# Gates of the mixer's merges as pairs of seven block products, and the modulation dots in the down parts

## The chip, the cores and the metric

The kernel runs on one core of one Trainium2 chip. The metric is the time of one execution on the device in microseconds (us). Before the change the median of three runs is 2345.42 us (2344.29 to 2346.27). A core has TensorE (PE, with its weight loads shown as PEld), VectorE (DVE), ScalarE (ACT), GpSimd (POOL) and SyncE (SP), which here issues nearly all DMAs. Each engine works off its own queue in order.

## The reference

Two layers, each of a feed-forward, a mixer and a second feed-forward on 512 tokens of 1024 channels in float32. Before each stands an RMS norm with a shift and a scale, behind it a gate, all three from `c @ w_ada + b_ada` (nine vectors of 1024 a layer, here called kinds 0 to 8: shift, scale, gate of each of the three sub-layers). The mixer, cut to what matters:

```python
proj = h @ w_in
qa, ka, va, ub, qc, kc, vc, f_lin, g_lin = jnp.split(proj, SPLIT_POINTS, axis=-1)
ya = chunked_relpos_attention(ha(qa), ha(ka), ha(va), qk_gain[0], qk_gain[1], rel_bias)
yb = multiscale_pool(ub, w_pool, pool_scale)          # windows 2, 4, 8, 16, one 128x128 map each
yc = forgetting_attention(hc(qc), hc(kc), hc(vc), qk_gain[2], qk_gain[3], f_lin + forget_bias)
ys = jnp.stack([ya, yb, yc], axis=2)
branch = jnp.einsum('bsnw,nwd->bsnd', ys, w_branch)   # three times 512 -> 1024
gates = jax.nn.sigmoid(g_lin.reshape(B, S, N_BRANCHES, D_MODEL))
merged = jnp.sum(gates * branch, axis=2)
return merged @ w_out
```

The gates `g_lin` are three products of 1024 x 1024 with the 512 tokens.

## The kernel before

**Precision.** Every large product is made from three matmuls (`triple`, L138): each operand is split into a high part, a copy to the matmul's float type by ScalarE, and a low part, the difference, by VectorE; high x high, high x low and low x high are added up in PSUM. A weight block of 128 x 1024 thus costs one ScalarE copy (L310) and one VectorE subtraction (L312), both in `wchunk`, which loads it through the tag "raw" (two buffers) and splits it into the tag "w" (three). The normed input is held split for good, as `hhi` and `hlo`: eight blocks of 128 channels by 512 tokens.

**Order.** The program is unrolled. A scheduler sets the order in each engine's queue from dependencies, free buffers and the order in which things are written. `later(delay, fn)` writes something down after so many 512-column matmuls of PE work (`pe`), at the next `poll`. `issue_after(ins)` puts an instruction behind `ins` on the same engine; `act_` and `vec_` chain everything that is passed to them in the written order on ScalarE and VectorE (`in_order`).

**Feed-forward.** 22 tiles of the hidden width are done in three parts of 6, 8 and 8. Where the gates and ups come in pairs of tiles, `stretch` computes them with the class `Seven` and `Blocks`: the weights of two tiles form a 2 x 2 block matrix (tile by half of the input channels), the input a 2 x 2 block matrix (half of the channels by half of the tokens), and seven block products with sums before and behind them replace eight (Strassen in Winograd's form). Each block product is `add_product` (L145), four times three matmuls of 256 columns. `Blocks` makes the sums of the input, `Seven` those of the weights: S1 and A11, S2, S3 and S4 and the second half, with their splits. Behind each gate and up part a down part follows (`k_outer`), in chunks of two tiles, for either half of the output.

**Modulation.** The rows of `w_ada` are loaded one by one (512 KB each, L220) and multiplied with the SiLU of c, spread over all partitions in `silc`, by one VectorE dot (L227). 16 rows are done at the start, 128 wait in `mod_queue`, in the order of the kinds. `side_work`, called with each weight chunk, adds `MOD_RATE` to a credit, and each whole credit draws a row, when `in_ffn` is set and the tag of the buffer, `mod_tag`, isn't "raw". `mod_need` draws what a later step needs at once. In `mod_dot` the dot is put behind the norm block written last (`after("norm")`), and the load behind the last weight load (`after("dma")`). Before, rows were drawn in the down parts (1.2 a chunk, into tag "v2") and in the merges of the mixer (1.2, into tag "b").

**Mixer.** Projections and the two attentions come first, with the attention branch's merge as filler of the second. Then `pool_in` projects the four groups of the pooling input; `pool_front` makes the window sums by doubling on VectorE, `pool_back` the small products. `merge_units` (L1217) goes through eight tiles of 128 output channels for the forgetting branch (n = 2) and eight for the pooling branch (n = 1): for each the gate, 8 x 3 matmuls of 512 columns, a tanh on ScalarE (L1238), the branch product, 4 x 3 matmuls, and `put_c` or `put_b`: VectorE multiplies (L1296), GpSimd adds to the merged block (L1297), and `put_b` also splits it for the output projection. That projection runs in two halves of four chunks; with its second half the next norm begins in two halves of the tokens (`Norm.front`, `Norm.back_start`, eight blocks `piece(d)` each, L404 to L407), while the first weights of the next feed-forward are loaded.

## Time and profile before

| | |
|---|---|
| median of three runs | 2345.42 us |
| the profiled execution | 2346.59 us |
| its span, first to last instruction | 2344.8 us |
| granted TensorE clock over the span | 1.000 |
| VectorE busy | 1749.1 us |
| dots of modulation rows into tag "b" (in the merges) | 57, 77.1 us of VectorE |
| dots into tag "v2" (start and down parts) | 87, 115.4 us of VectorE |
| GpSimd adds of the merges (L1297) | 32, 53.3 us |

The page sums the busy time of each engine over the span, and names groups of instructions by line, with count, sum and mean. Busy PE means that a matmul was under way; matmuls overlap at their ends, so the distance from start to start says what one costs in a stream. Views in order of time show start, length, engine, line and operands, and in brackets how long the engine was idle before and which instruction released it.

### The profile page before, as it was taken

Reading aid. Unit: us, or ns where it says so; the run is one execution under the profiler, and the core shown is the slowest. Engines: PE = TensorE matmul, PEld = TensorE weight load, DVE = VectorE, ACT = ScalarE, POOL = GpSimd, SP = SyncE. Lnnn points to the kernel's source line nnn. Section 1 sums busy time; section 2 is a strip of 40 time slices with the busy share of each in tenths; the row PEclk is TensorE's granted clock in tenths of the full one; section 3 lists DMA queues with packets and bytes.
Section 4 is the critical chain, followed back from the end, with each engine's and each line's share of the span. In section 5 each row is a group of like instructions: output and inputs, shape, how many; then the busy total and the mean of one; then the engine's idle time right before and its main releaser. Section 6 shows DMA issues by size and latency. Waiting matters only on the chain.

```text
span 2344.8 us, 37536 instructions
## 1 busy us (share of the span) xinstructions
PE 2315.3 (99%) x14322; PEld 2056.4 (88%) x14322; DVE 1749.1 (75%) x3042; ACT 1194.4 (51%) x2132; POOL 326.1 (14%) x433
## 2 busy tenths in 40 slices
PE   7999999999999999999999999999999999999999
PEld 5898998878888898989999989988788888999898
DVE  8887866787686577878687969677876865868593
ACT  5353555677632364635553636456765324636362
POOL 3000011244412110000000000112543112000000
PEclk9999999999999999999999999999999999999999
DMA  7625242333356524363325262533333655142322
GB/s 283 223 100 195 98 149 88 107 100 111 115 189 217 193 88 168 100 206 101 128 80 180 91 215 92 180 108 100 95 121 104 224 198 197 55 150 93 117 91 99
DMA packets 138137, 325.19 MB, mean 139 GB/s; under 512 B 13890, under 2 KB 16066, under 8 KB 137956
## 3 DMA queue, kind: packets, MB, share of 16 engines
q1 hardware_dynamic: 135266, 314.39, 39.7%
q0 software_dynamic: 2688, 8.39, 1.2%
q8 instruction: 113, 1.85, 0.3%
q14 instruction: 68, 0.56, 0.1%
q10 hardware_dynamic: 2, 0.00, 0.0%
HBM read 312.16 MB, written 6.38 MB: 136 GB/s over the span
## 4 chain that ended last, share of the span: by engine, by line
PE 50%; DVE 2%; ACT 2%; DMA 1%; issue 0%; POOL 0%; SPq 0%; ACTq 0%; DVEq 0%; POOLq 0%
PE acc L140 9%; PE acc L142 9%; PE acc L141 9%; PE acc L151 3%; PE acc L149 3%; PE acc L150 3%; PE mm L149 3%; PE mm L150 3%; PE mm L151 3%; PE mm L142 2%; PE mm L140 2%; PE mm L141 2%; PE mm L1111 0%; DVE w L312 0%; DMA v<-in_w_ada_dram 0%
## 5 line engine op out<-in xcount | busy, mean ns | idle before, releaser
L310 ACT CAST w<-raw 128x1024 fp32r<-128x1024 f32 (+1 forms) x255 | 264.4, 1041 | 268.1 <-PE acc L142 184.0
L312 DVE TENSOR_TENSOR w<-raw,w 128x1024 fp32r<-128x1024 f32 x247 | 312.8, 1270 | 116.6 <-ACT w L310 114.2
L140 PE MATMUL acc<-b,w 128*128 128x512 f32 (+1 forms) x960 | 360.1, 375 | 0.1
L142 PE MATMUL acc<-b,w 128*128 128x512 f32 (+1 forms) x960 | 356.4, 371 | 0.2 <-DVE w L312 0.2
L141 PE MATMUL acc<-b,w 128*128 128x512 f32 (+1 forms) x960 | 356.3, 371 | 0.0
L142 PEld LDWEIGHTS acc<-b,w 128*128 128x128 f32 x960 | 180.5, 188 | 32.3 <-DVE w L312 0.6
L140 PEld LDWEIGHTS acc<-b,w 128*128 128x128 f32 x960 | 180.4, 188 | 30.7 <-DVE xv L467 0.6
L141 PEld LDWEIGHTS acc<-b,w 128*128 128x128 f32 x960 | 180.4, 188 | 29.7
L140 PE MATMUL acc<-hhi,w 128*128 128x512 f32 x480 | 191.9, 401 | 2.5 <-ACT hhi L838 1.7
L142 PE MATMUL acc<-hhi,w 128*128 128x512 f32 x480 | 188.4, 393 | 2.0 <-DVE w L312 2.0
L141 PE MATMUL acc<-hlo,w 128*128 128x512 f32 x480 | 188.2, 392 | 2.1 <-DVE hlo L841 2.1
L140 PE MATMUL acc<-w,hhi 128*128 128x512 f32 x336 | 138.7, 414 | 0.9 <-ACT t L940 0.9
L142 PE MATMUL acc<-w,hlo 128*128 128x512 f32 x336 | 131.8, 392 | 0.0
L141 PE MATMUL acc<-w,hhi 128*128 128x512 f32 x336 | 131.7, 392 | 0.0
L227 DVE CUSTOM_DVE_ANT_0 v<-v,b,badac 128x1024 f32<-128x1024 f32 x87 | 115.4, 1339 | 17.1 <-DMA v<-in_w_ada_dram 17.1
L467 DVE SCALAR_TENSOR_TENSOR xv<-acc,badac,xv 128x512 f32<-128x512 f32 (+1 forms) x112 | 77.2, 690 | 67.7 <-PE acc L142 67.7
L557 DVE TENSOR_TENSOR ptb<-pta,ptb 128x1024 fp32r<-128x1024 f32 x70 | 85.7, 1224 | 50.9 <-ACT ptb L556 49.8
L149 PE MATMUL mm<-b,ptb 128*128 128x256 f32 x420 | 116.9, 278 | 1.8 <-ACT mm L610 1.8
L150 PE MATMUL acc<-b,ptb 128*128 128x256 f32 x420 | 116.1, 276 | 0.0
L151 PE MATMUL acc<-b,ptb 128*128 128x256 f32 x420 | 116.0, 276 | 0.0
L149 PE MATMUL acc<-b,ptb 128*128 128x256 f32 x420 | 116.0, 276 | 0.0
L150 PE MATMUL mm<-b,ptb 128*128 128x256 f32 x420 | 116.0, 276 | 0.0
(315 smaller groups left out, 6710.1 us busy)
## 6 DMA issues: line engine op xcount, KB each, us to landing
raw<-in_w_down_dram SPq DMA_DIRECT2D x88, 512.0 KB, 3.8
v<-in_w_ada_dram SPq DMA_DIRECT2D x87, 512.0 KB, 4.9
b<-in_w_ada_dram SPq DMA_DIRECT2D x57, 512.0 KB, 4.7
raw<-in_w_ubg_dram SPq DMA_DIRECT2D x56, 512.0 KB, 3.5
raw<-in_w_qkv_dram SPq DMA_DIRECT2D x42, 512.0 KB, 3.7
v<-in_w_gate_dram SPq DMA_DIRECT2D x70, 256.0 KB, 3.7
v<-in_w_up_dram SPq DMA_DIRECT2D x70, 256.0 KB, 3.2
raw<-in_w_gate_dram SPq DMA_DIRECT2D x70, 256.0 KB, 3.1
```

The costliest lines, as they stand in the source:

```text
L140: mm(o, lh, rh, start=start, stop=False)
L141: mm(o, lh, rl, start=False, stop=False)
L142: mm(o, ll, rh, start=False, stop=stop)
L149: mm(o, lh, rh, start=start and k == 0, stop=False, skip_group_check=True)
L150: mm(o, lh, rl, start=False, stop=False, skip_group_check=True)
L151: mm(o, ll, rh, start=False, stop=k == 3, skip_group_check=True)
L227: dot = nc.vector.tensor_tensor_reduce(out=raw, in0=raw, in1=silc[0], scale=1.0, scalar=badac[:, l, j, d:d + 1], op0=ALU.mult, op1=ALU.add ...
L310: nc.scalar.copy(hi, raw)
L312: lo_eng.tensor_tensor(lo, raw, hi.bitcast(F32), op=ALU.subtract)
L467: nc.vector.scalar_tensor_tensor(x, acc_j, gate, x, op0=ALU.mult, op1=ALU.add)
L557: vec_(lambda: nc.vector.tensor_tensor(pair[1], src, pair[0].bitcast(F32), op=ALU.subtract))
```

## The change

Per layer the gates of tiles 2 to 7 of the forgetting branch and of all eight tiles of the pooling branch are made in pairs by `merge_pairs`; tiles 0 and 1 of the forgetting branch stay with `merge_units`. `Blocks` is built while the pooling input is projected, and the first `Seven` during the direct tiles. The fronts and backs of the pooling groups are placed by hand: fronts between the two branch products of the first three pairs (`behind`), backs in the middle of the next pair's products (`between`), and all their VectorE and ScalarE steps are chained. No modulation rows are drawn in the merges; the down parts draw 1.9 a chunk, the last one 1.0 through the tag "pta" (one buffer), the mixer's projections 0.7, the output projection 1.0. Kind 7 comes ahead of kind 6, and `Ffn.run` asks for the shift of its norm itself. `silc` is loaded again behind the merges.

```diff
     def mod_step(l, j, d, tag="raw"):
-        raw = st([P, D], F32, tag, {"v2": 4, "raw": NRAW, "b": NB}[tag])
+        raw = st([P, D], F32, tag, {"v2": 4, "raw": NRAW, "b": NB, "pta": 1}[tag])
...
+    KINDS = (0, 1, 2, 3, 4, 5, 7, 6, 8)
...
-        return min(len(mod_queue), (l * 9 + j) * 8 + count - 16)
+        return min(len(mod_queue), (l * 9 + KINDS.index(j)) * 8 + count - 16)
...
         def run(self, nxt):
             l, s, ms = self.l, self.s, self.ms
+            if self.norm is not None:
+                mod_need(l, 3 * ms)
...
-                MOD_RATE[0] = 1.2
+                MOD_RATE[0] = 1.9
...
                         nxt.prefetch("v2")
-                        mod_tag[0] = "raw"
+                        mod_tag[0], MOD_RATE[0] = "pta", 1.0
...
     def pool_front(l, g, u):
...
-            nc.vector.tensor_tensor(nx[:, 16:], cur[:, 16:], cur[:, 16 - step:T + 16 - step], op=ALU.add)
+            vec_(lambda nx=nx, cur=cur, step=step: nc.vector.tensor_tensor(
+                nx[:, 16:], cur[:, 16:], cur[:, 16 - step:T + 16 - step], op=ALU.add))
...
-        b = st([P, 2, T], F32R, "ptb", 2)
-        split_to(b[:, 0, :], b[:, 1, :], df)
+        b = blk("b")
+        act_(lambda: nc.scalar.copy(b[:, 0, :], df))
+        vec_(lambda: nc.vector.tensor_tensor(b[:, 1, :], df, b[:, 0, :].bitcast(F32), op=ALU.subtract))
...
+    def merge_pairs(l, jobs, first, blocks):
...
+        todo = [first, Seven(gates(*jobs[1][:2]), ENTRY, stag="v2")]
+        for q, (n, d, ys, put, between, behind) in enumerate(jobs):
+            now = todo.pop(0)
+            nxt = todo[0] if todo else None
+            x, y, w = [acc((P, HALF)) for _ in range(3)]
...
+            go(x, "A11", "B11", True)
+            if nxt:
+                nxt.s1()
+            snap(y, x)
+            if nxt:
+                nxt.a11()
+                nxt.s234()
+            go(w, "S1", "T1", True)
+            snap(c[:, 2], w)
+            go(x, "S2", "T2", False)
+            snap(c[:, 0], x)
+            raw = st([P, 2, 4, P], F32, "raw", NRAW)
+            nc.sync.dma_start(raw, w_branch[l, n, d:d + 2].rearrange("a p k c -> p a k c"))
+            wb = duo((2, 4, P))
+            snap(wb[0], raw)
+            tens(wb[1], raw, wb[0].bitcast(F32), ALU.subtract)
+            if nxt:
+                nxt.pair12()
+            if q + 2 < len(jobs):
+                todo.append(Seven(gates(*jobs[q + 2][:2]), ENTRY, stag="v2"))
+            go(y, "A12", "B21", False)
+            go(x, "S3", "T3", False)
+            snap(c[:, 1], x)
+            for step in between:
+                step()
+            go(w, "S4", "B22", False)
+            tens(c[:, 1], c[:, 1], c[:, 2], ALU.add)
+            tens(c[:, 0], w, c[:, 0], ALU.add)
+            tanh(0, 0, y)
+            tanh(0, 1, c[:, 0])
+            if nxt:
+                nxt.pair34()
+            go(x, "A22", "T4", False)
+            tanh(1, 0, x)
+            tanh(1, 1, c[:, 1])
+            if nxt:
+                nxt.second()
+            for i in range(2):
+                pb = mmt()
+                for k in range(4):
+                    triple(pb, wb[0][:, i, k, :], wb[1][:, i, k, :], ys[k][:, 0, :], ys[k][:, 1, :], k == 0, k == 3)
+                put(d + i, pb, th[i])
+                if i == 0:
+                    for step in behind:
+                        step()
...
     class Mixer:
         def run(self, nxt):
-            in_ffn[0] = False
+            mod_tag[0], MOD_RATE[0] = "pta", 0.7
...
+            in_ffn[0] = False
             finish_turns()
...
             def put_b(d, pb, th):
                 put_c(d, pb, th)
-                b = blk("v2" if d < 4 else "b")
-                split_to(b[:, 0, :], b[:, 1, :], m[d // 2][:, d % 2, :])
-                mh.append(b)
+                if waiting:
+                    split_merged()
+                mh.append(blk("v2" if d == 5 else "b"))
+                waiting.append((m[d // 2][:, d % 2, :], mh[-1]))
...
+            blocks = Blocks()
+            blocks.schedule(4, 7)
+            us = [pool_in(l, gi) for gi in range(4)]
+            order.clear()
+            first = Seven([w_ubg[l, 4 + 2 * KD + 2 + i] for i in range(2)], ENTRY, "b", "v2")
+            for n, _ in enumerate(merge_units(l, 2, yc, put_c, 2)):
+                if n == 11:
+                    blocks.finish()
+                    first.prepare(first.pair34)
+            first.second()
...
+            jobs = [(2, 2, yc, put_c, [], [front(0), front(1)]), (2, 4, yc, put_c, [back(0), back(1)], [front(2)]),
+                    (2, 6, yc, put_c, [back(2)], [front(3)]), (1, 0, yb, put_b, [back(3)], [])]
+            jobs += [(1, d, yb, put_b, [], []) for d in (2, 4, 6)]
+            merge_pairs(l, jobs, first, blocks)
+            split_merged()
...
-            mc = merge_units(l, 2, yc, put_c)
...
-            in_ffn[0], mod_tag[0], MOD_RATE[0] = True, "b", 1.2
-            drain(mc)
-            poll(True)
-            mb = merge_units(l, 1, yb, put_b)
-            drain(mb)
-            in_ffn[0], mod_tag[0] = False, "raw"
...
+            in_ffn[0], mod_tag[0], MOD_RATE[0] = True, "pta", 1.0
             mod_need(l, 5)
```

64 lines of the change are left out of this document (39 added, 25 removed).

## The prediction

> **What bounds the kernel now.** I read the engine sums of the page first, then a table of busy time in stretches of 25 us, then the instructions in order of time inside the merges and inside a feed-forward part that already works with seven products.
>
> ```profile
> PE 2315.3 (99%) x14322; PEld 2056.4 (88%) x14322; DVE 1749.1 (75%) x3042; ACT 1194.4 (51%) x2132; POOL 326.1 (14%) x433
> ```
>
> TensorE is busy for 99% of the span, so its matmuls are the time, and anything else counts only where it makes TensorE wait. The merges lie, in the first layer, between about 667 us (first gate) and 801 us (last branch product).
>
> ```profile
> 700.00:725.00 25.00, 24.23 (x107) 19.66 (x106) 14.26 (x21) 6.08 (x8) 6.67 (x3) 1.00 0.62 216
> 975.00:1000.00 25.00, 25.00 (x223) 25.00 (x223) 23.19 (x33) 15.84 (x27) 0.00 (x0) 1.00 0.30 96
> 1250.00:1275.00 25.00, 25.00 (x112) 20.69 (x111) 22.34 (x44) 7.13 (x8) 0.00 (x0) 1.00 0.82 282
> 1800.00:1825.00 25.00, 24.76 (x117) 20.38 (x116) 16.80 (x29) 11.05 (x18) 2.44 (x9) 1.00 0.31 102
> ```
>
> Columns are stretch, length, then busy us and count of PE, PEld, DVE, ACT, POOL, the granted clock, DMA share and GB/s. In the pooling and merging stages only two stretches leave PE idle: 0.77 us and 0.24 us. I count 1.0 us of waiting there that the change may remove with the modulation dots. The second row is a seven-product part: VectorE busy for 23.2 of 25 us and no idle PE. So that scheme can run at 93% of VectorE, with everything in its fixed order.
>
> **What a matmul costs by its width.** Two streams without gaps, the first and last of 76 rows of 512 columns in the merges and of 117 rows of 256 columns in the seven-product part:
>
> ```profile
> 754.77 0.39 PE L141 MATMUL acc<-hlo,w 128*128 128x512 f32 x1
> ...
> 771.80 0.39 PE L141 MATMUL acc<-hlo,w 128*128 128x512 f32 x1
> ```
> ```profile
> 974.82 0.28 PE L151 MATMUL mm<-b,ptb 128*128 128x256 f32 x1
> ...
> 987.97 0.28 PE L150 MATMUL acc<-hlo,ptb 128*128 128x256 f32 x1
> ```
>
> Start to start that is 17.03 / 75 = 0.2271 us and 13.15 / 116 = 0.1134 us: half the width, half the time, although each matmul has its own weight load.
>
> **The saving.** A pair of gate tiles took 2 x 24 matmuls of 512 columns, 48 x 0.2271 = 10.90 us. It now takes 7 products x 12 matmuls of 256 columns, 84 x 0.1134 = 9.52 us. The branch product behind it stays at 24 x 0.2271 = 5.45 us. So 1.38 us a pair. A layer has three pairs of the forgetting branch and four of the pooling branch: 14 pairs, **-19.3 us**. One pair with its branch product should last 14.97 us.
>
> [...]
>
> **What the pairs put on VectorE.** Steps are taken start to start where instructions queue:
>
> ```profile
> 976.01 1.23 DVE L569 TENSOR_TENSOR pta<-v,raw 128x1024 f32<-128x1024 f32 x1
> 977.17 1.22 DVE L557 TENSOR_TENSOR ptb<-raw,ptb 128x1024 fp32r<-128x1024 f32 x1
> 984.21 0.68 DVE L560 TENSOR_TENSOR raw<-raw,v 128x512 f32<-128x512 f32 x1
> 984.82 0.69 DVE L557 TENSOR_TENSOR w<-raw,w 128x512 fp32r<-128x512 f32 x1
> 985.53 0.69 DVE L566 TENSOR_TENSOR raw<-raw 128x512 f32<-128x512 f32 x1
> 986.26 1.23 DVE L569 TENSOR_TENSOR pta<-v,raw 128x1024 f32<-128x1024 f32 x1
> 990.79 1.03 ACT L556 CAST ptb<-pta 128x1024 fp32r<-128x1024 f32 x1
> ```
>
> 1024 columns 1.15, 512 columns 0.61 (0.72 where the next needs the result), 256 columns 0.34; ScalarE 1024 columns 1.03. A pair's preparation is S1 0.61, low of A11 0.72, S2 0.73, S34 1.15, lows of the branch weights, of S1/S2, of the second half and of S3/S4 4 x 1.15, two sums 0.76, two products with the tanh 2 x 0.60: 9.8 us of 14.97. That alone would fit.
>
> The pooling work, unchained today, is put into the same fixed order, between the two branch products of a pair. One front in today's trace:
>
> ```profile
> 655.98 0.69 DVE L1188 TENSOR_TENSOR strip<-b 128x512 f32<-128x512 f32 x1 [2.13 <-ACT b L1178]
> 656.71 0.69 DVE L1188 TENSOR_TENSOR strip<-strip 128x512 f32<-128x512 f32 x1
> 658.45 0.17 DVE L1192 TENSOR_TENSOR hd<-strip,icnt 128x16 f32<-128x16 f32 x1
> 658.54 0.67 DVE L1194 SCALAR_TENSOR_TENSOR ssum<-strip,b 128x496 f32<-128x496 f32 x1
> 659.12 0.17 DVE L1195 TENSOR_TENSOR ssum<-hd,b 128x16 f32<-128x16 f32 x1
> 659.32 0.62 ACT L417 CAST ptb<-ssum 128x512 fp32r<-128x512 f32 x1 [2.42 <-DVE ssum L1195]
> ```
>
> Each of the g+1 adds takes 0.73, the three steps behind them 0.85, then ScalarE copies for 0.65 and VectorE takes 0.61 for the low part.
>
> And each `put` starts an add on GpSimd, which VectorE pays for:
>
> ```profile
> 684.40 1.23 DVE L312 TENSOR_TENSOR w<-raw,w 128x1024 fp32r<-128x1024 f32 x1 [1.49 <-ACT w L310]
> 687.62 2.33 POOL L1297 TENSOR_TENSOR xv<-xv,t 128x512 f32<-128x512 f32 x1 [7.94 <-DVE badac L238]
> 688.73 2.30 DVE L312 TENSOR_TENSOR w<-raw,w 128x1024 fp32r<-128x1024 f32 x1
> ```
>
> The same subtraction took 2.30 instead of 1.23 us beside the add. With VectorE behind, I charge 1.07 us for each of the two adds of a pair.
>
> **Where TensorE waits.** The second use of a pair's first accumulator (S2 onto x) must wait until ScalarE has copied x to y. That copy is queued on ScalarE behind the pooling copies of the pair before, which wait for VectorE; behind the copy stand the next A11 copy and all snapshots, so TensorE is held. PE wants S2 at 14.97 + 2 x 1.36 = 17.7 us after the first pair's start. When does the copy end? VectorE: product of the last direct tile, low of the second half, preparation up to the sums and one collision bring it to 9.25 us. ScalarE: a tanh 0.4, the S3/S4 copy 1.0, two tanh 0.65, the copy of the second half 1.0: 12.3. VectorE: low 1.15, product 0.60, front 0 1.58 + 1.07 + 0.65 + 0.61, front 1 2.31 + 0.65, then the copy 0.35: **21.3, a wait of 3.6 us**. Pair two: VectorE is free at 21.5; product, preparation, one collision and two pooled lows 9.3, ScalarE's steps 3.1, low and product 1.75, front 2 with a collision 4.1, copies 1.0: 40.8. PE, after its wait, wants it at 21.3 + 8.16 + 5.45 + 2.72 = 37.6: **3.2 us**. Pair three by the same steps, with one pooled low and front 3 (0.73 longer): 60.3 against 56.4, **3.9 us**. Pair four has no front: 0.5 us at most, through the new copies of the merged blocks. Pairs five to seven need about 15 us of the same loop, level with PE. Sum 11.2 a layer, **+22.4 us**.
>
> Bounds: with the adds on GpSimd costing nothing I get about 5 us a layer, and 2.4 if VectorE also starts each pair on time; with waits for the strip's memsets and full collisions 14.
>
> **The opening of the pairs.** While the four pooled inputs (21.8 us of PE) and two direct tiles (16.4 us) run, VectorE must make the block sums (four 1024-column sums, eight 512-column differences, four lows, about 16 us by the steps above), seven lows of weights 8 us, and the first pair's preparation 6.6 us with its two products and collisions 3.4 us: 34 of 38 us, with one of the two raw buffers held by the first pair. I take 0.5 us a layer, **+1.0 us**, bounds 0 and 3 a layer.
>
> **The dots moved.**
>
> ```profile
> L227 DVE CUSTOM_DVE_ANT_0 b<-b,b,badac 128x1024 f32<-128x1024 f32 x57 | 77.1, 1360 | 36.2 <-DMA b<-in_w_ada_dram 36.1
> b<-in_w_ada_dram SPq DMA_DIRECT2D x57, 512.0 KB, 4.7
> ```
>
> 57 rows leave the merges. The down parts draw 1.9 instead of 1.2 a chunk. A chunk is 24 matmuls, 5.45 us; in it VectorE needs one low 1.15, 1.9 dots of 1.4 and about 0.8 for the residuals: 4.6. The queue moves 2.9 x 0.524 MB in 5.45 us, 279 GB/s; the third row of the first table had 282 GB/s and no idle PE. I cost this part **0**.
>
> The start of the second feed-forward is another matter. Counting the draws of the first layer: 6 before the first down part, 11.4 and 15.2 in two of them, 4 in the last, 2.8 in the mixer's projections, one that the prefetch asks for, 4 in the output projection: 44. The new `mod_need` there asks for 48, the shift of the third norm; in the second layer it is 116 of 120. Four rows are left, for blocks 4 to 7, all through the one buffer "pta", so each load waits for the dot before it. And a dot is written behind the norm block that was written last (`after("norm")`), which at that place is block 3.
>
> ```profile
> 845.67 0.28 PE L140 MATMUL mm<-hhi,ptb 128*128 128x256 f32 x1
> 845.73 0.87 DVE L407 SCALAR_TENSOR_TENSOR hlo<-b,badac,hhi 128x256 fp32r<-128x256 f32 x2
> 849.01 0.37 PE L140 MATMUL mm<-hhi,b 128*128 128x256 f32 x1
> 849.34 0.28 PE L141 MATMUL mm<-hlo,ptb 128*128 128x256 f32 x1
> 854.55 1.28 DVE L407 SCALAR_TENSOR_TENSOR hlo<-b,badac,hhi 128x256 fp32r<-128x256 f32 x3
> ```
>
> Blocks 2 and 3 are done at 846.6 today. From there the four dots end at 848.0, 854.1, 860.2 and 866.3 (1.4, then three times 4.7 + 1.4), and block 7 follows about 1 us later, at 867.3. PE starts the feed-forward at 845.67; a block's share for one half is 9 matmuls of 256 columns, 1.02 us. If PE takes what is ready, blocks 0 to 4 of the first half last until 850.8, and then nothing is there until the second half's blocks come at about 855: **4 us a layer, +8 us**. That it takes work out of turn is in the rows: the third unit's matmul (weights in b) stands at 849.01 among those of the first two (weights in ptb). If it kept strictly to the written order it would stand at block 5 from 849, with 8 x 0.68 us of first and second unit done only after 867: 17 us a layer. If the loads could be drawn ahead of block 3, it were 0. I keep both as ends.
>
> **Sum.** -19.3 - 1.0 + 22.4 + 1.0 + 8 = +11.1 us. The profiled execution took 2346.59 us (span 2344.8 and 1.8 around it), 1.2 above the median of the runs, 2345.42. So 2357.7 for such an execution, and **2356.5 us** on the scale of the median.
>
> **Rivals.**
> - *The pooling work is hidden.* If GpSimd's adds fall beside ScalarE's steps, the waits in the pairs are 5 us a layer: 2356.5 - 12.4 = 2344 us, no change. For it: the seven-product part at 93% of VectorE has no idle PE. Against: there only a pair's own steps stand before the copy of x, and GpSimd has 0.00 us in that row.
> - *The late rows are hidden*, because VectorE and the queue take them ahead: 2356.5 - 8 = 2348.5 us, no change. With both hidden, 2336 us: faster, and the change then gives about what its matmuls say.
> - *The late rows hold PE to the written order.* 17 instead of 4 us a layer: 2356.5 + 26 = 2382 us. It decides from the point at which the four dots stand in VectorE's queue ahead of the second half's blocks.
> - *Weight loads set the pace.* A load lasts 188 ns; were it the step of a narrow matmul, a pair would cost 84 x 0.188 - 10.90 = +4.9 us and the time were 2345 + 69 = 2414. The stream of 0.1134 us speaks against it. [...]
>
> ```profile
> L142 PEld LDWEIGHTS acc<-b,w 128*128 128x128 f32 x960 | 180.5, 188 | 32.3 <-DVE w L312 0.6
> ```
>
> **How the numbers follow.** Forecast 0.42; pooling hidden alone 0.13; late rows hidden alone 0.15; both 0.17; written order 0.12; weight loads 0.01. A measurement tells about 0.2%, 4.7 us, from no change. The forecast with the bounds of the opening and of the pairs reaches from 2350 to 2366, slower; the two single hidings are no change, both together faster, the rest slower: 0.17, 0.28, 0.55. The range reaches from 2337, about the case of both hidden, to 2370, a third of the way to the written order.
>
> **What would show it.** Right: in the first three pairs of each layer PE is idle for 3 to 4 us each, ended by ScalarE's copy of x, which stands behind a pooling copy that waits for VectorE; the later pairs last 15 us; and some microseconds into the second feed-forward PE is idle with a dot or its load behind the releaser. Wrong: no idle PE in the pairs, rows of the third norm's shift that land before 846, or narrow matmuls over 0.12 us apart.

## The result and the profile after

The changed kernel takes **2398.24 us** (median of four runs, 2394.82 to 2399.33), the kernel before 2345.85 us beside it. The ratio is **1.022, with an interval of 1.020 to 1.024**: 52 us slower. The forecast was 2356.5 us, its range ended at 2370: the direction was right, the size was not.

The engine sums on the page of the changed kernel:

```profile
span 2397.6 us, 38927 instructions
PE 2323.3 (97%) x14826; PEld 2082.2 (87%) x14826; DVE 1850.8 (77%) x3172; ACT 1242.2 (52%) x2252; POOL 323.8 (14%) x433
```

The span is 52.8 us longer. TensorE is idle for 74.3 instead of 29.5 us, and it is busy for 8.0 us more, although its matmuls should have lost 19.3 us. So there are two questions: where it waits, and why it is slower while it works. The table by stretches of 25 us (same columns as before the change) bears on both:

```profile
700.00:725.00 25.00, 23.34 (x144) 20.47 (x143) 20.69 (x28) 11.53 (x21) 3.69 (x5) 1.00 0.29 93
725.00:750.00 25.00, 20.12 (x132) 18.60 (x131) 21.14 (x29) 9.28 (x18) 5.57 (x8) 0.93 0.26 85
850.00:875.00 25.00, 20.09 (x147) 19.06 (x145) 20.17 (x64) 11.22 (x27) 2.72 (x4) 0.85 0.20 62
875.00:900.00 25.00, 22.60 (x133) 20.37 (x132) 18.45 (x28) 14.09 (x20) 0.00 (x0) 0.87 0.28 86
1250.00:1275.00 25.00, 25.00 (x189) 23.75 (x188) 17.83 (x20) 13.13 (x23) 0.00 (x0) 1.00 0.26 88
```

The third number from the end of a row, the granted clock, counts: before the change it was 1.00 in all rows shown. Now it is 0.93 in the pairs and 0.85 and 0.87 at the start of the second feed-forward, stretches in which PE has idle time (the first row has some too, at a clock of 1.00). Between 28 and 2396 us the profile's record of the clock has it at 0.50 in seven stretches, 40.9 us in all. TensorE works in 32.4 us of them, and at the full clock that work would take at most 16.2 us less, half of it (an estimate from the clock of 0.50). So of the 27.3 us by which its busy time lies above 2315.3 - 19.3, the clock explains up to 16; the other 11 were not taken apart. The list of PE's waits (total, times, longest) names what it waited for:

```profile
PE mm L140 <- ACT hhi L407: 15.1, 6, 3.1
PE acc L149 <- ACT acc L1260: 11.8, 6, 3.1
PE acc L140 <- ACT w L311: 6.9, 4, 3.2
PE mm L140 <- ACT w L311: 4.0, 3, 3.3
```

In this order: the normed blocks of the second feed-forward; the copy of x to y in the pairs, as forecast; the weights of a direct gate in the opening; the last weights of the output projection.

The whole difference can be cut at marker instructions, whose times in one profile are set against those in the other. The markers are the first copy of a pooled input (`pool_in`), the first and the last `put` of the forgetting and pooling branches, the first matmul of the second feed-forward, and the Silu of its last direct unit. For that last stage the first marker of the kernel before, at 845.67, stands in the prediction; its second one and both of the changed kernel are these:

```profile
885.56 0.60 ACT L687 ACTIVATE t<-mm 128x512 f32<-128x512 f32 x1 [1.24 <-PE mm L142]
```
```profile
858.99 0.28 PE L140 MATMUL mm<-hhi,ptb 128*128 128x256 f32 x1
910.88 0.60 ACT L688 ACTIVATE t<-mm 128x512 f32<-128x512 f32 x1 [1.30 <-PE mm L142]
```

The stage took 39.89 us before and takes 51.89 us now. All stages measured so, first and second layer, in us:

| stage | before | changed | difference | forecast, both layers |
|---|---|---|---|---|
| opening, to the first put | 27.33, 28.27 | 30.44, 28.69 | +3.1, +0.4 | +1.0 |
| rest of the merges, to the last put | 123.98, 122.11 | 126.34, 127.74 | +2.4, +5.6 | +2.1 (-19.3 - 1.0 + 22.4) |
| output projection | 44.44, 44.76 | 49.82, 46.16 | +5.4, +1.4 | 0 |
| start of the second feed-forward | 39.89, 39.86 | 51.89, 52.10 | **+12.0, +12.2** | +8 |
| all else (down parts, projections, attention) | | | +10.3 in all | 0 |

3.5 + 8.0 + 6.8 + 24.2 + 10.3 = 52.8. One profile of each kernel stands behind these figures, and a stage with the same code differs between profiles: the opening lasts 28.6 to 31.6 us in the changed kernel and in e1, e2, e4, e5 and e11 below, which have it in common.

### The profile page after: what moved, and what is told of

Read it like the earlier page. It is cut to its first block, busy times and chain, and to the rows that moved or that the text cites. A ratio compares the mean times of both kernels' runs of the same rounds, so it can differ in the third digit from the quotient of the medians.

```text
span 2397.6 us, 38927 instructions
## 1 busy us (share of the span) xinstructions
PE 2323.3 (97%) x14826; PEld 2082.2 (87%) x14826; DVE 1850.8 (77%) x3172; ACT 1242.2 (52%) x2252; POOL 323.8 (14%) x433
## 4 chain that ended last, share of the span: by engine, by line
PE 70%; DVE 15%; DMA 6%; ACT 5%; issue 3%; SPq 0%; POOL 0%; DVEq 0%; ACTq 0%; POOLq 0%
PE acc L140 9%; PE acc L142 9%; PE acc L141 9%; PE acc L149 6%; PE acc L151 6%; PE acc L150 6%; PE mm L149 4%; PE mm L151 4%; PE mm L150 4%; PE mm L140 3%; PE mm L142 3%; PE mm L141 3%; DVE v L227 3%; DVE w L313 2%; DMA raw<-in_w_down_dram 2%
## 5 line engine op out<-in xcount | busy, mean ns | idle before, releaser
L311 ACT CAST w<-raw 128x1024 fp32r<-128x1024 f32 (+1 forms) x213 | 220.5, 1039 | 268.6 <-PE acc L142 119.6
L140 PE MATMUL acc<-b,w 128*128 128x512 f32 (+1 forms) x896 | 333.1, 372 | 1.4 <-DVE badac L238 1.2
L142 PE MATMUL acc<-b,w 128*128 128x512 f32 (+1 forms) x896 | 329.2, 367 | 2.8 <-DVE w L313 2.8
L141 PE MATMUL acc<-b,w 128*128 128x512 f32 (+1 forms) x896 | 328.8, 367 | 0.0
L313 DVE TENSOR_TENSOR w<-raw,w 128x1024 fp32r<-128x1024 f32 x205 | 250.5, 1226 | 101.2 <-ACT w L311 100.7
L142 PEld LDWEIGHTS acc<-b,w 128*128 128x128 f32 x896 | 168.5, 188 | 32.9 <-DVE w L313 4.5
L140 PEld LDWEIGHTS acc<-b,w 128*128 128x128 f32 x896 | 168.3, 188 | 29.4 <-DVE badac L238 2.1
L141 PEld LDWEIGHTS acc<-b,w 128*128 128x128 f32 x896 | 168.4, 188 | 26.3
L149 PE MATMUL acc<-b,ptb 128*128 128x256 f32 x588 | 164.5, 280 | 11.8 <-ACT acc L1260 11.8
L151 PE MATMUL acc<-b,ptb 128*128 128x256 f32 x588 | 164.0, 279 | 0.0
L150 PE MATMUL acc<-b,ptb 128*128 128x256 f32 x588 | 163.9, 279 | 0.0
L227 DVE CUSTOM_DVE_ANT_0 v<-v,b,badac 128x1024 f32<-128x1024 f32 x109 | 142.9, 1328 | 9.5 <-DMA v<-in_w_ada_dram 9.4
L558 DVE TENSOR_TENSOR ptb<-pta,ptb 128x1024 fp32r<-128x1024 f32 x70 | 85.7, 1224 | 50.9 <-ACT ptb L557 49.8
L149 PEld LDWEIGHTS acc<-b,ptb 128*128 128x128 f32 x588 | 111.6, 190 | 13.1 <-ACT acc L1260 13.0
L149 PE MATMUL mm<-b,ptb 128*128 128x256 f32 x420 | 116.8, 278 | 1.8 <-ACT mm L611 1.8
L150 PE MATMUL mm<-b,ptb 128*128 128x256 f32 x420 | 116.0, 276 | 0.0
L151 PE MATMUL mm<-b,ptb 128*128 128x256 f32 x420 | 116.0, 276 | 0.0
L140 PE MATMUL acc<-hhi,w 128*128 128x512 f32 x256 | 105.6, 415 | 8.6 <-ACT w L311 6.9
L558 DVE TENSOR_TENSOR w<-v,w 128x1024 fp32r<-128x1024 f32 x82 | 100.1, 1220 | 16.6 <-ACT w L557 16.6
```

The costliest lines, as they stand in the source:

```text
L140: mm(o, lh, rh, start=start, stop=False)
L141: mm(o, lh, rl, start=False, stop=False)
L142: mm(o, ll, rh, start=False, stop=stop)
L149: mm(o, lh, rh, start=start and k == 0, stop=False, skip_group_check=True)
L150: mm(o, lh, rl, start=False, stop=False, skip_group_check=True)
L151: mm(o, ll, rh, start=False, stop=k == 3, skip_group_check=True)
```

## The experiments

Twelve kernels were run, each beside the kernel before. The theory after the result: the pairs cost what was forecast; most of the loss is the rows that are late at the second feed-forward, made worse because TensorE runs at half its clock there (0.50 from 867.64 to 881.29 us) behind idles of 2.00 to 2.90 us; the rest is queues in front of the opening and the output projection. The rivals: it is the pairs that cost more, or the dots cost the same wherever they stand.

| run | median us | ratio to before, interval |
|---|---|---|
| changed kernel | 2398.2 | 1.0221, 1.0204 to 1.0239 |
| e1_four_buffers | 2381.2 | 1.0150, 1.0135 to 1.0165 |
| e2_copy_behind | 2408.6 | 1.0270, 1.0255 to 1.0285 |
| e3_dots_only | 2377.1 | 1.0135, 1.0119 to 1.0150 |
| e4_fill | 2396.4 | 1.0217, 1.0203 to 1.0230 |
| e5_wout_rows | 2379.0 | 1.0145, 1.0128 to 1.0162 |
| e6_first_later | 2388.0 | 1.0181, 1.0167 to 1.0195 |
| e8_add_on_vector | 2393.8 | 1.0202, 1.0188 to 1.0216 |
| e9_pooling_pairs | 2350.6 | 1.0019, 1.0011 to 1.0028 |
| e10_three_repairs | 2367.8 | 1.0089, 1.0076 to 1.0103 |
| e11_one_add | 2389.8 | 1.0184, 1.0170 to 1.0198 |
| e12_pooling_pairs_late | 2349.1 | 1.0011, 1.0002 to 1.0020 |
| e13_pooling_pairs_vector | 2343.5 | 0.9986, 0.9977 to 0.9995 |

### The dots alone

The kernel before, with the hunks of the change that move the rows, and the merges left as they were:

```diff
-                MOD_RATE[0] = 1.2
+                MOD_RATE[0] = 1.9
...
-                        mod_tag[0] = "raw"
+                        mod_tag[0], MOD_RATE[0] = "pta", 1.0
...
-            in_ffn[0], mod_tag[0], MOD_RATE[0] = True, "b", 1.2
             drain(mc)
```

> The kernel before with the moved dots alone: merges as before, but no dots in them; draws of 1.9 in the down parts, of 0.7 to 1 in projections and output projection; kinds in the new order; shift rows asked for at the start of the second feed-forward. Theory (most of the loss is the moved dots: second feed-forward 24, output projection 6, down parts and the rest about 8 us, less 2 us of waits in the merges): 2346 + 36 = about 2382 us (2374 to 2390). Rival (the dots are cheap and it is the pairs that cost, through the clock or GpSimd): under 2360 us. Rival of the prediction on record (late rows 8 us, all else free): 2353 us.

2377.1 us, as the theory had it, and 24 us above what the prediction on record gives for it. The start of the second feed-forward lasts 51.9 and 52.3 us in this kernel too, and there are no pairs in it. So 24.5 of the 30.5 us by which its span is longer are the late rows, without any help of the pairs. The stages under "all else" are 5.2 us longer here.

### The late rows

The changed kernel at that place: the queue of SP, then VectorE's dots, then PE, from three timelines.

```profile
861.64 11.12 SPq L220 DMA_DIRECT2D pta<-in_w_ada_dram  x3
```
```profile
860.23 1.38 DVE L227 CUSTOM_DVE_ANT_0 pta<-pta,b,badac 128x1024 f32<-128x1024 f32 x1
865.20 1.28 DVE L227 CUSTOM_DVE_ANT_0 pta<-pta,b,badac 128x1024 f32<-128x1024 f32 x1 [0.27 <-DMA pta<-in_w_ada_dram]
869.71 1.08 DVE L405 TENSOR_TENSOR b<-acc,b 128x256 f32<-128x256 f32 x3 [1.77 <-PE acc L399]
871.12 1.28 DVE L227 CUSTOM_DVE_ANT_0 pta<-pta,b,badac 128x1024 f32<-128x1024 f32 x1
875.81 1.28 DVE L227 CUSTOM_DVE_ANT_0 pta<-pta,b,badac 128x1024 f32<-128x1024 f32 x1
```
```profile
867.09 0.50 PE L140 MATMUL mm<-hhi,ptb 128*128 128x256 f32 x2 [2.00 <-ACT hhi L407]
873.00 0.80 PE L140 MATMUL mm<-hhi,ptb 128*128 128x256 f32 x2 [2.90 <-ACT hhi L407]
877.70 0.80 PE L140 MATMUL mm<-hhi,ptb 128*128 128x256 f32 x2 [2.40 <-ACT hhi L407]
```

The dots stand 5.0, 5.9 and 4.7 us apart, each load behind the dot before it, as forecast, though that had them 6.1 us apart. And PE waits behind the second, third and fourth of them: block 5, 6 and 7 of the first half. The second half's blocks begin on VectorE at 869.71 (L405), and ScalarE makes three and three of them in these rows:

```profile
870.17 1.31 ACT L407 ACTIVATE hhi<-b,badac 128x256 fp32r<-128x256 f32 x3 [3.14 <-DVE b L405]
874.08 1.29 ACT L407 ACTIVATE hhi<-b,badac 128x256 fp32r<-128x256 f32 x3
```

VectorE has finished their low parts by 875.89. Yet PE stands idle until 877.70, and no matmul of the second half starts before the first half is through, at 879.79: TensorE kept to the order of its queue here.

One line gives the rows four buffers:

```diff
             if self.norm is not None:
+                mod_tag[0] = "v2"
                 mod_need(l, 3 * ms)
```

> One line: the four late rows of the shift at the start of the second feed-forward are loaded into the four "v2" buffers instead of the one "pta". Theory (late rows: each load waits for the dot before it, PE stands idle, and the idle drops the granted clock to 0.5): the last dot moves from about 877 to about 865 us, the idle of 2.0 + 2.9 + 2.4 us there goes, and with it the low clock: 8 to 10 us a layer, 2398 - 18 = about 2380 us (2376 to 2386). Rival (the dots are late because they stand behind norm block 3, whatever the buffers): under 4 us, 2394 us or more. Rival (the clock drops there through the idle in the output projection): idle goes, clock stays at 0.85 in 850 to 875 us, 2390 us.

2381.2 us, as expected. The stage lasts 45.8 and 44.6 us: half of the loss there is gone. The other half is that the four dots still come together behind norm block 3: in the first layer they stand one after another from 857.04 to 862.36, and PE waits 2.46 us for the block behind them. Drawing the rows earlier removes all of it:

```diff
-            in_ffn[0], mod_tag[0], MOD_RATE[0] = True, "pta", 1.0
+            in_ffn[0], mod_tag[0], MOD_RATE[0] = True, "v2", 2.0
             mod_need(l, 5)
```

> In the output projection the rows are drawn at 2.0 a chunk into the four "v2" buffers, instead of 1.0 into the one "pta": 48 rows are then drawn before the second feed-forward, so none is late, and SyncE's queue is not held by a load that waits for the one buffer. Theory (late rows cost 12 us a layer with the clock, the held queue 3 to 4): 2398 - 28 = about 2370 us (2364 to 2378). Rival (the dots cost the same wherever they are made, VectorE in the output projection is then late): 2388 us or more. Rival (only the late rows matter, the last weights of the output projection come as late as now): about 2376 us, with PE's wait of 3.3 us at the last chunk of the output projection still there.

The stage lasts 39.98 and 39.98 us, 0.1 above the kernel before. But the time, 2379.0 us, missed the expected range by 1 us, since the output projection grew: it lasts 52.1 and 51.0 us, with nine and eight dots in it. PE still waits for the last weights there, 2.70 and 2.13 us, so the rival by which only the late rows matter came nearest, and other buffers for the rows did not keep this stage short. With five and four dots through one buffer the stage lasts 49.8 and 46.2 us in the changed kernel, but 46.8 and 44.6 in e3; in e9 below, with none, it lasts 44.60 and 44.61, the time of before. So a row drawn there costs between nothing and 1.1 us. What sets this price stays open, and so does the part that the held queue of SP has in it.

### Idle time or clock

What the granted clock does, in steps of 2 us of the changed kernel (length, PE busy, clock, DMA share, GB/s):

```profile
864.00:866.00 2.00, 1.09 (x10) 1.00 0.24 96
866.00:868.00 2.00, 0.91 (x5) 0.91 0.24 49
868.00:870.00 2.00, 2.00 (x8) 0.50 0.53 213
872.00:874.00 2.00, 1.00 (x4) 0.50 0.31 78
878.00:880.00 2.00, 2.00 (x10) 0.50 0.04 8
880.00:882.00 2.00, 2.00 (x14) 0.68 0.23 29
882.00:884.00 2.00, 2.00 (x20) 1.00 0.81 297
```

Behind the first wait the clock is halved: ten matmuls in 2 us instead of twenty. By the record of the clock it stays so from 867.64 to 881.29; the windows at both times stand in the last section. e4 keeps TensorE busy instead, with work that nobody uses, ahead of each of the three blocks:

```diff
                             self.unit(pu, u0, cols, (k,))
+                            if hs == 0 and s == 1 and 4 <= k < 7:
+                                fill = acc()
+                                for _ in range(14):
+                                    with tc.issue_after(newest[0]):
+                                        newest[0] = mm(fill[:, cols], g0[0][:, 0, :], hhi[:, 0, cols], ...)
```

> The changed kernel with 14 matmuls of 256 columns, whose result nobody uses, ahead of the blocks 5, 6 and 7 of the first half in the second feed-forward: TensorE is kept busy for 1.6 us of each of the three waits there, and the chain of loads and dots is untouched. Theory (an idle of 2 to 3 us drops the granted clock to 0.5, and the work behind the last wait runs at half speed): the clock stays above 0.9 in 858 to 892 us, and the time falls by 2 to 4 us a layer although TensorE does 84 matmuls more, to 2391 to 2395 us. Rival (the low clock lies beside waits that bind anyway): clock at 1.00 and the time unchanged, 2397 to 2400 us. Rival (the clock drops for another reason than the idle): it is at 0.5 there again.

The same table of e4:

```profile
868.00:870.00 2.00, 0.87 (x8) 1.00 0.01 2
874.00:876.00 2.00, 0.83 (x5) 1.00 0.00 0
878.00:880.00 2.00, 2.00 (x19) 1.00 0.00 0
```

The clock stays at 1.00 throughout the stage, with 1.13 and 1.17 us of idle left in the first two rows: where the waits are filled, the halving is gone. The stage lasts 49.3 and 49.4 us, 2.6 less a layer than in the changed kernel, though TensorE does 9.5 us more work in the two layers: the clock is about 2.6 of the 12 us, the rest is waiting for the rows. In the whole time the gain, 1.9 us, lies inside the spread of the runs, and the median lies just outside the expected 2391 to 2395; only the stage shows it.

### The pairs

The times of ScalarE's copy of x to y, by the timeline of ScalarE, first layer:

```profile
691.62 0.36 ACT L1260 COPY acc<-acc 128x256 f32<-128x256 f32 x1 [1.93 <-PE acc L151]
710.69 0.37 ACT L1260 COPY acc<-acc 128x256 f32<-128x256 f32 x1
730.03 0.37 ACT L1260 COPY acc<-acc 128x256 f32<-128x256 f32 x1
749.55 0.37 ACT L1260 COPY acc<-acc 128x256 f32<-128x256 f32 x1
765.55 0.37 ACT L1260 COPY acc<-acc 128x256 f32<-128x256 f32 x1
780.20 0.36 ACT L1260 COPY acc<-acc 128x256 f32<-128x256 f32 x1
795.42 0.36 ACT L1260 COPY acc<-acc 128x256 f32<-128x256 f32 x1 [0.77 <-PE acc L151]
```

The periods are 19.07, 19.34, 19.52, 16.00, 14.65 and 15.22 us. For comparison, two direct tiles with one pooling product would take 75 x 0.2271 = 17.0 us, an estimate from the step of the wide matmuls in the prediction. From the rows around the second copy one sees what holds it: VectorE's last difference of the window, ScalarE's copy of it, the copy of x, and then PE.

```profile
709.97 0.17 DVE L1201 TENSOR_TENSOR ssum<-hd,b 128x16 f32<-128x16 f32 x1
710.17 0.62 ACT L1203 CAST b<-ssum 128x512 fp32r<-128x512 f32 x1 [2.97 <-DVE ssum L1201]
710.69 0.37 ACT L1260 COPY acc<-acc 128x256 f32<-128x256 f32 x1
711.11 0.38 PE L149 MATMUL acc<-b,ptb 128*128 128x256 f32 x1 [0.99 <-ACT acc L1260]
```

Three experiments tell what sets these periods. First, the window sums cut to one add each (the kernel leaves out the other adds, and the GpSimd memset that goes with each), all else the same:

```diff
-        while step < w:
+        while step < 2:
```

> The changed kernel with only the first add of each pooling window (the others are left out: one fewer in the first pair, two in the second, three in the third, 0.73 us each on VectorE). Theory of the record (VectorE's chain up to ScalarE's copy of x sets the period of these pairs): the periods fall from 19.07, 19.34 and 19.52 us to about 18.3, 17.9 and 17.3 us, PE's waits there to 0.2, 1.7 and 0.3 us, and with the clock the time to 2398 - 10 = about 2388 us (2385 to 2392). Rival (the wait for GpSimd's memsets and adds, or ScalarE's own queue, sets the period): the periods fall by less than half of that, 2394 us or more.

2389.8 us; the periods are 18.35, 17.81 and 17.13 us, each within 0.2 of the expected. VectorE's chain sets them, add by add. It isn't the memsets of 0.11 us: in the changed kernel's trace no more than 0.12 us lies between one sum of a window and the next on VectorE. At the third pair the wait only changed its place: PE now waits there for a pooling product's input, 2.03 us (L1203), instead of 1.75 us for the copy of x.

Second, GpSimd's add of `put_c` put on VectorE:

```diff
-                nc.gpsimd.tensor_tensor(md, md, tmp, op=ALU.add)
+                vec_(lambda: nc.vector.tensor_tensor(md, md, tmp, op=ALU.add))
```

> The add of put_c goes from GpSimd to VectorE, in its fixed order (14 adds a layer in the pairs, 2 before them). Theory (VectorE as a whole bounds pairs one to three, and an add on GpSimd lengthens the VectorE instruction beside it by 1.07 us, more than the 0.61 us it takes itself): the periods of 19.1, 19.3 and 19.5 us fall by 0.5 to 1 us each, with the clock 2398 - 5 = about 2393 us (2389 to 2396). Rival (the lengthening is harmless or the add on VectorE costs as much): 2397 us or more.

2393.8 us; the periods are 18.46, 18.78 and 19.34 us, 0.6, 0.6 and 0.2 shorter, the third by less than expected. The add is cheaper on the full engine, where it takes 0.69 us, than on GpSimd, where a VectorE subtraction beside it took 1.1 us longer (rows in the last section).

Third, ScalarE's copy of the pooled differences behind the copy of x, so that the chain above no longer stands in front of it (`sums` makes the window sums of a group, `fin` ScalarE's copy of the differences and their low part):

```diff
-            jobs = [(2, 2, yc, put_c, [], [front(0), front(1)]), (2, 4, yc, put_c, [back(0), back(1)], [front(2)]),
-                    (2, 6, yc, put_c, [back(2)], [front(3)]), (1, 0, yb, put_b, [back(3)], [])]
+            jobs = [(2, 2, yc, put_c, [], [front(0), sums(1)]),
+                    (2, 4, yc, put_c, [fin(1), back(0), back(1)], [sums(2)]),
+                    (2, 6, yc, put_c, [fin(2), back(2)], [sums(3)]), (1, 0, yb, put_b, [fin(3), back(3)], [])]
```

> The pooling sums stay between the branch products of a pair, but ScalarE's copy of the differences (and its low part) is written into the next pair, behind its copy of x to y and in front of the pooling product. Theory (ScalarE's copy of x to y is held by the pooling copy that waits for VectorE): PE's waits for acc at pairs two to four (1.0, 3.1 and 1.8 us a layer in the changed kernel) fall below 1 us each, and the clock stays at 1.00 there: 5 us a layer of idle and 1.7 us of clock, 2398 - 13 = about 2385 us (2381 to 2390). Rival (VectorE as a whole is full in these pairs, its order does not matter): the wait moves to another row of the same pairs, 2394 us or more.

2408.6 us: a miss, and slower than the change. The wait moved to other rows of the same pairs, as the rival had it. At pairs two to four PE no longer waits for the copy of x (a wait of 1.92 us for it stands at pair five), but others, longer, came in its place (PE's timeline of this kernel):

```profile
730.03 0.39 PE L151 MATMUL acc<-hhi,w 128*128 128x256 f32 x1 [2.28 <-DVE w L558]
752.24 0.58 PE L151 MATMUL acc<-hhi,w 128*128 128x256 f32 x1 [4.28 <-DVE w L558]
```

L558 makes the low part of the next pair's A11, and it is queued on VectorE behind the window sums. The copy and its low part, now in the middle of the next pair, stand ahead of the pooling product, for which VectorE waits in its turn. So moving the copy does not free the time. Since its low part on VectorE moved with it, e2 doesn't tell which of the two moves did the harm. That it is the sums in VectorE's fixed order which cost the time is shown by e11, and fits e9 below, whose pairs have no sums between them and last 15.2 to 15.3 us.

### The opening, and all repairs together

In the opening the first pair's weights hold one of the two raw buffers, and the weights of the direct gates are left with the other. e6 loads them one gate later:

```diff
-            first = Seven([w_ubg[l, 4 + 2 * KD + 2 + i] for i in range(2)], ENTRY, "b", "v2")
             for n, _ in enumerate(merge_units(l, 2, yc, put_c, 2)):
+                if n == 0:
+                    first = Seven([w_ubg[l, 4 + 2 * KD + 2 + i] for i in range(2)], ENTRY, "b", "v2")
```

> The weights of the first pair are loaded after those of the first direct gate, instead of ahead of them, so that the second raw buffer is free for the gate. Theory (the first gate waits for the one raw buffer that is left): PE's wait of 3.2 and 2.9 us at the first direct gate falls under 1 us, with the clock (0.96 and 0.97 in two stretches there): 2398 - 7 = about 2391 us (2388 to 2395). Rival (VectorE is late there by its sums for the blocks): the wait stays or the first pair begins later by as much, 2396 us or more.

2388.0 us, 10 us less, at the lower end of the expected range. The wait for the gate's weights is gone, and the opening lasts 24.59 and 24.58 us instead of 30.44 and 28.69. Part of this comes back behind the opening: from the first copy of a pooled input to the last put the merges are 4.0 and 3.8 us shorter.

e10 has the edits of e5, e6 and e8 together:

> The rows in the output projection through four buffers, the first pair's weights later, and the adds of put_c on VectorE, together, all seven pairs a layer kept. Theory (the three losses lie in different stages and add up): 2398 - 19 - 10 - 4.5 = about 2364 us (2360 to 2369), still slower than before; PE's waits that are left are those for ScalarE's copy of x in pairs two to four and 2 to 3 us at the last chunk of the output projection. Rival (part of them is the same loss, seen twice): 2370 us or more.

2367.8 us: they add up, within 4 us. What is left is 21 us above the kernel before. Its merges, from the first copy of a pooled input to the last put, last 151.2 and 150.5 us, before the change 151.3 and 150.4: the seven pairs of a layer should save 9.7 us, but the first four periods sum to 73.0 us, where four pairs of 14.97 us with a pooling product each would be 62.6, with PE's waits of 1.0, 2.5 and 2.7 us for the copy of x still among them. Of the 18.3 us by which its profiled span is longer than before, 11.1 lie in the output projection with its rows (50.1 and 50.2 us), and 7.2 in all else.

### Pairs only where no window sums stand

The later pairs last about 15.2 us a piece. So e9 keeps only the four of the pooling branch; the forgetting branch is direct again, with the pooling work beside it in no fixed order, and eight rows are drawn there instead of four in the output projection:

```diff
+            chained[0] = False
...
+            for gi in range(4):
+                us.append(pool_in(l, gi))
+                later(28, lambda gi=gi: pooled(gi))
+            in_ffn[0], mod_tag[0], MOD_RATE[0] = True, "v2", 1.6
...
-            jobs += [(1, d, yb, put_b, [], []) for d in (2, 4, 6)]
+            jobs = [(1, d, yb, put_b, [], []) for d in (0, 2, 4, 6)]
```

> Only the four pairs of the pooling branch are merged by seven products; all eight tiles of the forgetting branch are direct, with the pooling work beside them unchained as before, 8 rows a layer drawn beside the first three direct tiles, and none in the output projection; the rest of the rows in the down parts as in the change, none late at the second feed-forward. Theory (pairs without a pooling front last 15 us, and the dots in the down parts cost about 1 us): 2346 - 2 x 4 x 1.38 + 3 to 5 = about 2339 us (2335 to 2345), faster than both. Rival (the opening of the pairs and the last chunks of the output projection cost their 3 us a layer wherever the pairs begin): 2347 us or more.

2350.6 us, above the rival's 2347: from the first copy to the last put the merges gained 1.5 us a layer, not 5.5, in good part since the gates waited for weights beside VectorE's block sums (1.7 and 1.6 us in the first layer), and all other stages together are 8 us longer. e12 starts the block sums later and draws more rows beside the direct tiles, fewer in the down parts (1.75):

> The kernel with pairs in the pooling branch alone, its sums for the blocks begun 9 units later in the direct tiles, 13 to 15 rows a layer drawn there at 2.0 a chunk, and 1.75 instead of 1.9 in the down parts. Theory (VectorE's bunch of sums and dots makes the direct gates wait, 3 us a layer, and each tenth in the down parts costs some 0.8 us in all): 2350.6 - 5 = about 2345 us (2341 to 2349), the time of before. Rival (VectorE is full in the direct tiles, wherever sums and dots are put): 2350 us or more.

2349.1 us: just past the upper edge and below the rival's 2350, so the two cannot be told apart. Waits of 1.9 and 1.5 us a layer stayed, in other places, and the merges last 151.0 and 151.8 us, no less than before the change. e13 takes the adds to VectorE, and the pooling products 12 units later:

> The kernel before this one (pairs in the pooling branch alone, sums for the blocks late), with the adds of put_c on VectorE instead of GpSimd, and the pooling products 12 units later. Theory (its waits of 1.9 and 1.5 us a layer, for the low part of a pooled block and of a gate's weights, come from VectorE, slowed by adds on GpSimd, and from a pooling product that stands too early in TensorE's order): both waits go, 2349.1 - 5 = about 2344 us (2340 to 2347), just under before. Rival (VectorE is full in the direct tiles and the wait moves to another low part): 2348 us or more.

**2343.5 us, ratio 0.9986 (0.9977 to 0.9995)**: the one version that is below both kernels, by 0.14%, which is little more than the measurement tells. Its merges are 4.7 and 3.1 us shorter than before, of the 5.5 that four pairs can give, and in this profile the other stages take all of it back: its span is 0.7 us longer than before (it is the longest of the eleven executions). The kernel before with its adds on VectorE, and no pairs, was not run, so how much of the gain is the pairs' and how much the adds' stays open.

## Why the prediction was wrong

**Right: the matmuls, and what holds the pairs.** Pairs without pooling work last 14.65 to 15.30 us against the forecast 14.97, so half the width costs half the time here as well (from 858.99 to 861.71 in the changed kernel 24 steps at 256 columns take 0.1133 us each, beside 0.2271 at 512). The holder, ScalarE's copy of x behind a pooling copy that waits for VectorE, is in the rows, and e11 confirms the chain add by add. The price of 1.07 us for a GpSimd add is confirmed too (1.78 - 0.69 below).

**Right in part by luck: the size of the loss in the pairs.** The first four periods of the first layer sum to 73.93 us; four pairs of 14.97 with one pooling product each (3 x 0.2271) are 62.6, so 11.3 us are lost, against 11.2 forecast; in the second layer 12.1. But the forecast was made of PE's waits for the copy of x, 3.6, 3.2 and 3.9 us, and the rows have 1.0, 3.1 and 1.8, 5.9 in all. Of the other 5.4 the clock at 0.50 for 3.41 us from 731.11 is 1.7 at most; the rest was not taken apart. Two slips stand in the forecast's own sum. It leaves out the pooling products that PE does in the pairs, 0.68 us each, by which PE asks for the copy later and waits less. And by its own step, 40.8 + 8.16 + 5.45 + 2.72, PE wants the third copy at 57.1 and not at 56.4, a wait of 3.2 us. The merges behind the opening came out 5.9 us dearer than forecast (8.0 instead of 2.1), of which the pairs' loss, 23.4 instead of 22.4, is 1.0; for the rest no cause was found.

**Wrong: the start of the second feed-forward, 8 forecast, 24.2 measured.** The cause was named rightly, down to the four rows, the one buffer and the block behind which the dots stand. The step that failed is "if PE takes what is ready, blocks 0 to 4 of the first half last until 850.8, and then nothing is there until the second half's blocks come at about 855". Here PE did not take what was ready: with six blocks of the second half done at 875.89 it stayed idle until 877.70, for the last block of the first half. The matmul that stood out of turn at 849.01 is no sign that it does: the scheduler of the program sets the order of each queue when the kernel is built, and can have given it that place. In the changed kernel the second half stands behind the whole first half, and nothing filled the gaps between the dots. The case lies between the forecast (4 us a layer) and the rival of the written order (17): 12 us, of which the clock is about 2.6.

**Wrong: an idle was counted at its own length.** No term allowed for the halved clock behind it (0.50 for 13.65 us from 867.64). The view of the cores puts the mean clock at 0.991 of full speed instead of 1.000. Of the 16.2 us that this adds at most to TensorE's work, only what lies outside other waits costs time: by e4 2.6 us a layer at the second feed-forward. In the pairs one stretch can be read by itself: in the second layer the clock is at 0.50 for 3.41 us from 1936.01, and the fourth period is 16.89 us there, against 16.00 in the first layer without it, 0.9 us.

**Wrong: the opening, 1.0 forecast, 3.5 measured** in this profile, more in others of the same opening. By e6 the place of the first pair's weights costs 5.9 and 4.1 us of the opening, and 4.0 and 3.8 us of the merges as a whole. The prediction had seen that one raw buffer is held, but priced only VectorE's load.

**Wrong: the output projection, 0 forecast, 6.8 measured.** The term "4 in the output projection" was counted as a draw of rows and not as work in a stage. With no rows the stage lasts what it did before (44.6 us), with four or five 44.6 to 50.1, with eight or nine 50.1 to 52.1.

**Wrong in part: the dots in the down parts and elsewhere, 0 forecast, 10.3 measured in this profile, 5.2 in e3.** The down parts have PE waits of about 1 us for a low part behind a dot. In the ten other kernels with 1.9 rows a chunk, "all else" is 5.2 to 7.7 us longer than before, but 14.0 in e4. So 5 to 8 us go with the dots, and the rest of the 10.3 probably with this one execution: the stages up to the first pooled input have the same code in nine of these kernels, and end between 650.2 and 652.4 us, in the changed kernel last of all.

In sum: 16.2 too little at the second feed-forward, 5.9 in the merges, 2.5 in the opening, 6.8 in the output projection and 10.3 elsewhere are 41.7 us; with the 11.1 forecast that is the 52.8.

## What to carry to other kernels

Work that is moved off a stage that has no idle time must be followed to every place where it lands: buffers, queues and the instructions behind it there, each with a price of its own; e3 shows that here the move alone cost 31 us, and made the merges that it freed 1.4 us shorter. In the changed kernel PE stood idle until 877.70 beside six blocks that were done at 875.89, so look up what stands behind the waiting instruction in the built order rather than what is ready. And when TensorE's saving is paid with work on an engine that already runs at 80% (VectorE, 20.69 and 21.14 of 25 us beside the window sums), put it where that engine has no second client. A pair without window sums lasts about 15.2 us, less than the 16.4 of two direct tiles (an estimate, 72 x 0.2271); the three pairs beside the sums last 19.1 to 19.5, more than the 17.0 of two direct tiles with a pooling product. That the four good pairs alone make the whole kernel faster is not shown: e9 and e12 are not faster than the kernel before, and e13 has its adds on VectorE as well.

## What the runs showed of the hardware

In the changed kernel's trace the granted clock changes fourteen times between 60 and 2320 us, and these times lie whole numbers of 3.41 us apart: it goes down at 867.64 and up at 881.29, four times 3.41 us later, and down at 1936.01 and up at 1939.43. In the trace of the kernel before it stays at 1.00 over the same stretch. Cut into windows of 3.41 us at these times, the changed kernel's trace has seven at the full clock behind which it dropped to 0.50, and in each of them TensorE was idle for at least 1.88 us in sum; in the others at the full clock it was idle for at most 1.75 us. The clock came back behind seven windows with at most 0.48 us of idle, and stayed at 0.50 behind five with at least 0.95 us. The same count over the fourteen traces has 60 windows ahead of a drop, with at least 1.75 us of idle, 9093 others at the full clock with at most 1.88 us, 60 ahead of the return with at most 0.52 us, and 43 with that much or more behind which it stayed at 0.50. These are counts; what sets the clock no trace shows. Windows of the changed kernel, then of e8:

```profile
864.23:867.64 3.41, 1.41 (x12) 1.00 0.16 38
867.64:871.05 3.41, 2.46 (x9) 0.50 0.36 144
877.88:881.29 3.41, 3.41 (x17) 0.50 0.03 5
881.29:884.70 3.41, 3.41 (x31) 1.00 0.80 267
```
```profile
1926.86:1930.27 3.41, 1.84 (x15) 1.00 0.00 0
1930.27:1933.68 3.41, 3.41 (x28) 1.00 0.02 5
```

The length of one idle alone doesn't tell these cases apart: behind one of 1.88 us, which ended at 1935.45 in the changed kernel, the clock was 0.50, and behind one of 1.92 us in e8, which ended at 1928.43, it stayed at 1.00. Of the latter 0.35 us lay in the window before.

Beside an add on GpSimd of 1.68 us a VectorE subtraction took 1.78 us, 1.1 us longer than one of the same shape without an add beside it (0.69, L1204 at 710.82):

```profile
712.18 1.68 POOL L1371 TENSOR_TENSOR xv<-xv,t 128x512 f32<-128x512 f32 x1 [1.90 <-DVE t L1370]
712.63 1.78 DVE L558 TENSOR_TENSOR w<-raw,w 128x512 fp32r<-128x512 f32 x1
```

In e8 VectorE does the add itself in 0.69 us, and the first three periods are 0.2 to 0.6 us shorter.
